# Folding the row maxima of four query tiles at once, one causal mask for both orientations, and smaller tiles for the norm weights, in a hybrid attention block

## The chip, the cores and the metric

The kernel runs on one core of a Trainium2 chip. The time is that of one execution on the device in microseconds; the kernel before was run three times, and the median of the runs counts. One more execution was recorded by the hardware profiler.

## The reference

One layer of a decoder trunk over 2048 tokens of width 1024. A normed input is projected once; its columns feed three attention branches and a gate. The branches' outputs, times the gate, go through one output projection and are added to the input.

```python
h = rms_norm(x, norm_g)
cq, ckv, kr, dq, dk, dv, mq, z = split(h @ w_in)
# A: latent attention, 8 heads, q and k of 64 + 32 (rotary) columns, causal
q = rms_norm(rms_norm(cq, q_norm_g) @ w_uq, qn_g); k = rms_norm(concat(k_nope, kr), kn_g)
a = softmax(where(causal, rope(q) @ rope(k).T / sqrt(96), -1e30)) @ v
# B: differential attention, 4 heads, two maps of 32 columns each, causal
p = softmax(where(causal, q @ k.T / sqrt(32), -1e30))
b = rms_norm((p[0] - lam * p[1]) @ v, subln_g) * (1 - lam_init)
# C: cross-attention to 256 memory tokens, 4 heads
c = softmax(rms_norm(mq, qn_g) @ rms_norm(k_mem, kn_g).T / sqrt(64)) @ v_mem
out = x + (concat(a, b, c) * silu(z)) @ w_out
```

## The kernel before

Everything is computed in tiles of 128 tokens, four of them to a block of 512, four blocks in all. Values that need more precision than 16 bits are kept as a high and a low 16-bit part, so that projections and scores take two or three matmuls each.

The work is cut into **steps**: one per branch, head group and block (`m` for memory, `d` for differential with 2 groups, `a` for latent with 4 groups; 4 blocks each). A step has two parts. Its **preparation** (`prep_m`, `prep_d`, `prep_a`) projects, norms and turns the queries and keys, and ends with an estimate of the row maxima (`est_block`). Its **maps** (class `Map`) then run over key tiles: scores into PSUM on TensorE, exponential on ScalarE (L506), the low part of the probabilities on VectorE (L507), and the product with the values on TensorE (L516, L518, L536).

`est_block` is what the change touches most. For each map of a pair of heads, and for each of four query tiles `t`, it multiplies the queries with the high parts of all keys so far, one block `c` of up to 512 keys at a time (L398). On the diagonal block a second matmul adds the causal mask (L400). From block 1 on (`fold`), ScalarE copies the scores to SBUF in bf16: the first block of keys goes straight to the tile `er` (L404), each later one to a tile `ec` (L407), which VectorE merges into `er` by a maximum (L408). `er` holds two query tiles and has one buffer. After each pair of query tiles VectorE folds the 512 columns to 256, 128 and 64 (L412) and reduces the 64 (L413). When all are there, the maxima are scaled by -1/32 on VectorE (L421) into a spare column of the query tile, which SyncE then turns by a transposing DMA (L484, L900). The scores of the maps read that turned tile, so that the exponential needs no further shift.

```python
                if fold and t % 2:
                    for n in (256, 128, 64):
                        V.tensor_tensor(er[:, :, 0:n], er[:, :, 0:n], er[:, :, n:2 * n], ALU.max)
                    V.reduce_max(mx[:, m, t - 1:t + 1, 0], er[:, :, 0:64], axis=AX.X)
```

Two masks are kept: `mask_t` (keys in rows) is added to the scores of the maps (L575, L921), and `mask_e`, its transpose, to the estimates. Norm weights lie as rows broadcast to all partitions (`gain_row`, L83): `g_mk` and `g_mq` for memory, `g_q` and `g_k` of 96 columns for the latent branch, whose first 64 are only used in a product `g_n`. Small sums and inverse norms (`ss`, and `rstd_of` on GpSimd, L91) have two buffers each; the rotary tables times gain (`rt`) have one.

The order of the instructions on each engine is not that of the program. A loop at the end of the kernel takes the next piece of a preparation, a filling task (gates, latents, output projection) or a map by a table of costs and due times, and gives each a priority. A scheduler with a model of the engines' times then sets the order on each engine, so that an edit in one place can move instructions elsewhere.

## Time and profile before

| | |
|---|---|
| three runs | 1371.38, 1371.22, 1367.65 us; median 1371.22 us |
| profiled execution | 1372.15 us, its span 1370.3 us |
| matmuls on TensorE | busy 94% of the span, weight loads 61% |
| VectorE, ScalarE, GpSimd | busy 82%, 66%, 24% |
| granted TensorE clock | 0.989 of full speed, mean over the span |

The span runs from the first to the last instruction. An engine's share is an average over stages with different limits. The chain of waits follows the work that ended last back to what released it, so its shares say on which engines the end depended; work of an engine that is not on it lay beside other work.

### The profile page before, as it was taken

The numbers are of one execution on the slowest core, as the hardware profiler recorded it, in microseconds if no ns is written. First come the engines' busy times: TensorE is split into PE (matmuls) and PEld (weight loads), VectorE is DVE, ScalarE is ACT, GpSimd is POOL, SyncE is SP. The second block draws the span as 40 slices with busy tenths as digits, with TensorE's granted clock in tenths as the row PEclk, the third lists the DMA queues.
The fourth block names the chain that finished last, engine by engine and source line by source line (L and its number), as shares of the span: only waits on it lengthen the run. The fifth ranks groups of instructions, "written<-read, shape, count | busy, mean of one in ns | idle before, by whom it ended". The sixth has DMA issues, their size and how long they took to land.

```text
span 1370.3 us, 35041 instructions
## 1 busy us (share of the span) xinstructions
PE 1293.0 (94%) x13616; PEld 829.5 (61%) x13616; DVE 1123.1 (82%) x2713; ACT 903.9 (66%) x2163; POOL 333.9 (24%) x477
## 2 busy tenths in 40 slices
PE   5988999999999999999998999999999998999998
PEld 2434556667667767667775656666655665655554
DVE  4657888879889867889899889999998998886745
ACT  6656544677878646786896667677766877665521
POOL 2322232403042133113202143223243323200000
PEclk9999999999999999999999999999999999999999
DMA  7998844223113322447446166347525643275452
GB/s 231 199 208 184 184 111 101 59 60 88 41 25 71 79 34 60 78 110 193 124 98 144 40 167 150 84 107 167 109 71 118 145 99 55 40 155 158 141 184 70
DMA packets 294262, 155.52 MB, mean 113 GB/s; under 512 B 239952, under 2 KB 272848, under 8 KB 294096
## 3 DMA queue, kind: packets, MB, share of 16 engines
q1 hardware_dynamic: 294064, 153.29, 47.7%
q8 instruction: 106, 1.74, 0.5%
q14 instruction: 60, 0.49, 0.1%
q0 software_dynamic: 32, 0.00, 0.0%
HBM read 61.75 MB, written 34.34 MB: 70 GB/s over the span
## 4 chain that ended last, share of the span: by engine, by line
PE 56%; DVE 13%; POOL 9%; ACT 8%; DMA 8%; issue 4%; SPq 1%; ACTq 0%; DVEq 0%; POOLq 0%
PE pp L189 6%; PE pp L187 6%; PE pp L188 6%; PE pe L398 5%; DVE plo L507 4%; PE pv L518 3%; PE pv L516 3%; PE pv L536 3%; PE st L572 3%; PE pp L958 3%; PE pp L959 3%; PE pp L960 3%; PE st L917 3%; PE st L918 2%; PE st L919 2%
## 5 line engine op out<-in xcount | busy, mean ns | idle before, releaser
L506 ACT ACTIVATE p<-st 128x512 f32<-128x512 f32 (+3 forms) x672 | 356.2, 551 | 167.2 <-PE st L919 65.8
L507 DVE TENSOR_TENSOR plo<-p 128x512 f16<-128x512 f32 (+3 forms) x672 | 404.6, 615 | 63.1 <-ACT p L506 59.2
L407 ACT ACTIVATE ec<-pe 128x512 bf16<-128x512 f32 (+3 forms) x384 | 197.2, 536 | 39.2 <-PE pe L400 17.1
L516 PEld LDWEIGHTS <-p 128*128 128x128 bf16 x2304 | 186.0, 99 | 51.5 <-DVE y_a L924 4.7
L518 PEld LDWEIGHTS <-p 128*128 128x128 bf16 x2304 | 173.1, 98 | 39.4 <-issue 4.1
L408 DVE TENSOR_TENSOR er<-er,ec 128x512 bf16<-128x512 bf16 (+3 forms) x384 | 141.5, 378 | 29.9 <-ACT ec L407 15.2
L404 ACT ACTIVATE er<-pe 128x512 bf16<-128x512 f32 x192 | 110.0, 606 | 47.2 <-DVE mx_a L413 18.1
L536 PEld LDWEIGHTS <-plo 128*128 128x128 f16 x2304 | 123.1, 97 | 23.7 <-DVE plo L507 5.8
L917 PE MATMUL st<-qB_a,kT_a 97*128 97x512 f16 (+1 forms) x320 | 112.8, 353 | 13.6 <-ACT p L506 8.7
L516 PE MATMUL pv<-V_d,p 128*128 128x65 f16 x1088 | 116.8, 194 | 3.3 <-DVE y_d L579 2.9
L189 PEld LDWEIGHTS <-ht_x 128*128 128x128 f16 x896 | 87.7, 98 | 52.9 <-ACT ht_x L137 3.9
L188 PEld LDWEIGHTS <-ht_x 128*128 128x128 f16 x896 | 87.8, 98 | 47.8 <-issue 4.0
L518 PE MATMUL pv<-V_d,p 128*128 128x64 f16 x1088 | 116.5, 196 | 0.0
L572 PE MATMUL st<-qB_d,kT_d 97*128 97x512 f16 (+1 forms) x320 | 111.4, 353 | 5.2 <-ACT zc L704 2.1
L187 PEld LDWEIGHTS <-ht_x 128*128 128x128 f16 x896 | 87.7, 98 | 47.1 <-issue 2.8
L516 PE MATMUL pv<-V_a,p 128*128 128x65 f16 x1088 | 112.6, 193 | 2.0 <-DVE y_a L924 1.9
L918 PE MATMUL st<-qB_a,kT_a 96*128 96x512 f16 (+1 forms) x320 | 112.6, 352 | 0.0
L398 PE MATMUL pe<-kT_d,qB_d 96*128 96x512 f16 (+2 forms) x320 | 106.2, 348 | 6.8 <-ACT ec L407 3.6
L518 PE MATMUL pv<-V_a,p 128*128 128x64 f16 x1088 | 112.2, 195 | 0.0
L919 PE MATMUL st<-qB_a,kT_a 96*128 96x512 f16 (+1 forms) x320 | 111.9, 350 | 0.0
L398 PE MATMUL pe<-kT_a,qB_a 96*128 96x512 f16 (+2 forms) x320 | 100.0, 349 | 7.7 <-DMA qB_a<-qs_a 4.6
L189 PE MATMUL pp<-w_d,ht_x 128*128 128x512 f16 x256 | 97.0, 379 | 0.0
(293 smaller groups left out, 3337.7 us busy)
## 6 DMA issues: line engine op xcount, KB each, us to landing
xt_x<-in_x_dram SPq DMA_DIRECT2D x16, 512.0 KB, 4.7
xr<-in_x_dram SPq DMA_DIRECT2D x16, 512.0 KB, 3.6
part<-xr SPq DMA_DIRECT2D x16, 512.0 KB, 2.9
ysc<-yt SPq DMA_DIRECT2D x31, 256.0 KB, 2.3
yl<-ysc SPq DMA_DIRECT2D x15, 512.0 KB, 4.6
zsc<-zc SPq DMA_DIRECT2D x48, 128.0 KB, 2.1
xa<-part SPq DMA_DIRECT2D x12, 512.0 KB, 3.6
out_dram<-xa SPq DMA_DIRECT2D x12, 512.0 KB, 2.9
```

The source lines that it names most:

```text
L187: T.matmul(ps[:, :n], lhsT=ht[:, 0, k], rhs=wt[:, 0, :n], start=(k == 0), stop=False)
L188: T.matmul(ps[:, :n], lhsT=ht[:, 0, k], rhs=wt[:, 1, :n], start=False, stop=False)
L189: T.matmul(ps[:, :n], lhsT=ht[:, 1, k], rhs=wt[:, 0, :n], start=False, stop=(k == NK - 1))
L398: T.matmul(ps[:, 0:n], lhsT=lhs(m, t), rhs=rhs(m, c, n // P), start=True, stop=c < b)
L407: A.activation(ec[:, 0:n], ps[:, 0:n], AF.Copy)
L506: A.activation(p32[:, :n], ps[:, :n], AF.Exp, scale=self.scale)
L507: V.tensor_tensor(plo[:, :n], p32[:, :n], phi[:, :n], ALU.subtract)
L516: T.matmul(pvv[:, t, 0:65], lhsT=phi[:, c], rhs=vt[:, 0:65], start=(j == 0 and t == 0), stop=False, skip_group_check=True)
L518: T.matmul(pvv[:, t, 0:64], lhsT=phi[:, c], rhs=vt[:, 65:129], start=False, stop=False, skip_group_check=True)
L536: last["pv"] = T.matmul(pvv[:, t, 0:65], lhsT=plo[:, c], rhs=vt[:, 0:65], start=False, stop=(j == self.njt - 1), skip_group_check=True)
L572: T.matmul(ps[:, :n], lhsT=st.kTs[j // 4][0:97, h, j % 4, m % 2, :], rhs=st.qB[h][0:97, t0:4, m % 2, :], start=True, stop=not diag)
L917: T.matmul(ps[:, :n], lhsT=kt[0:97, h, j % 4, 0, :], rhs=q[0:97, 0, t0:4, :], start=True, stop=False)
```

## The change

- `er` holds four query tiles instead of two (4 KB a partition instead of 2 KB) and is folded once per map, after its last query tile; the three maxima and the reduction are twice as wide and half as many.
- The scaling of the maxima by -1/32 is done on ScalarE (an activation with a scale) instead of VectorE.
- `mask_e` is gone: on the diagonal block `mask_t` is loaded as weights and the identity is streamed, where the identity was loaded and `mask_e` streamed.
- The memory branch's two gains share one tile, which takes the rotary table's buffer (`rtab`); the latent branch's gains keep only the 32 rotary columns, and the product `g_n` is made from a 64-column row and one in a temporary tile.
- `ss` and the inverse norms of tag `rstd` have one buffer instead of two.

```diff
-    mask_e = cst.tile([P, P], BF16, name="mask_e")
-    make_causal_mask(nc, mask_e, mask_val=NEG)
...
-        r = sm.tile([P, 32 if tag == "rstd" else 8], F32, tag=tag, name=name)
+        r = sm.tile([P, 32 if tag == "rstd" else 8], F32, tag=tag, name=name, bufs=1 if tag == "rstd" else 2)
...
-    g_mk = gain_row(mem_kn_g, 64, "g_mk")
-    g_mq = gain_row(mem_qn_g, 64, "g_mq")
-    V.tensor_tensor(g_mk, g_mk, g_mq, ALU.mult)
+    g_m2 = wk.tile([P, 2, 64], F32, tag="rtab", name="g_m2", bufs=1)
+    SP.dma_start(g_m2[:, 0], mem_kn_g.broadcast_to([P, 64]))
+    SP.dma_start(g_m2[:, 1], mem_qn_g.broadcast_to([P, 64]))
+    g_mk = g_m2[:, 0]
+    V.tensor_tensor(g_mk, g_mk, g_m2[:, 1], ALU.mult)
...
-    g_q = gain_row(mla_qn_g, 96, "g_q")
-    g_k = gain_row(mla_kn_g, 96, "g_k")
-    g_n = cst.tile([P, 64], F32, name="g_n")
-    V.tensor_tensor(g_n, g_q[:, 0:64], g_k[:, 0:64], ALU.mult)
+    g_q = gain_row(mla_qn_g[:, 64:96], 32, "g_q")
+    g_k = gain_row(mla_kn_g[:, 64:96], 32, "g_k")
+    g_n = gain_row(mla_qn_g[:, 0:64], 64, "g_n")
...
+    SP.dma_start(lamw[:, 192:256], mla_kn_g[:, 0:64].broadcast_to([P, 64]))
+    V.tensor_tensor(g_n, g_n, lamw[:, 192:256], ALU.mult)
...
-                if fold and t % 2 == 0:
-                    er = wk.tile([P, 2, 512], BF16, tag="er", name="er", bufs=1)
+                if fold and t == 0:
+                    er = wk.tile([P, 4, 512], BF16, tag="er", name="er", bufs=1)
...
-                        T.matmul(ps[:, t * P:n], lhsT=ident, rhs=mask_e, start=False, stop=True)
+                        T.matmul(ps[:, t * P:n], lhsT=mask_t, rhs=ident, start=False, stop=True)
...
-                        A.activation(er[:, t % 2], ps, AF.Copy)
+                        A.activation(er[:, t], ps, AF.Copy)
...
-                        V.tensor_tensor(er[:, t % 2, 0:n], er[:, t % 2, 0:n], ec[:, 0:n], ALU.max)
+                        V.tensor_tensor(er[:, t, 0:n], er[:, t, 0:n], ec[:, 0:n], ALU.max)
...
-                if fold and t % 2:
-                    for n in (256, 128, 64):
-                        V.tensor_tensor(er[:, :, 0:n], er[:, :, 0:n], er[:, :, n:2 * n], ALU.max)
-                    V.reduce_max(mx[:, m, t - 1:t + 1, 0], er[:, :, 0:64], axis=AX.X)
+            if fold:
+                for n in (256, 128, 64):
+                    V.tensor_tensor(er[:, :, 0:n], er[:, :, 0:n], er[:, :, n:2 * n], ALU.max)
+                V.reduce_max(mx[:, m, :, 0], er[:, :, 0:64], axis=AX.X)
...
-            V.tensor_scalar_mul(mcol(m), mr[:, m, :], -1.0 / MS)
+            A.activation(mcol(m), mr[:, m, :], AF.Copy, scale=-1.0 / MS)
...
-        ss = sm.tile([P, 32], F32, tag="ss", name=f"ss_{nm}")
+        ss = sm.tile([P, 32], F32, tag="ss", name=f"ss_{nm}", bufs=1)
```

The scheduler writes the order anew. Three places follow. The first is VectorE at the end of the first folded estimate of the latent branch (group 0, block 1, first head), `plo` being the low part of the probabilities and `mx` the maxima. Before:

```order
L526 RECIPROCAL rl<-pv 128x4
L412 TENSOR_TENSOR er<-er 128x2x256
L581 TENSOR_SCALAR rl<-rl,neglam 128x4
L412 TENSOR_TENSOR er<-er 128x2x128
L583 SCALAR_TENSOR_TENSOR y_d_11718<-pv,rl,y_d_11718 128x64 x4
L412 TENSOR_TENSOR er<-er 128x2x64
L413 TENSOR_REDUCE mx_a_13330<-er 128x2
L408 TENSOR_TENSOR er<-er,ec 128x384
L408 TENSOR_TENSOR er<-er,ec 128x512
L507 TENSOR_TENSOR plo<-p_12559 128x512
L412 TENSOR_TENSOR er<-er 128x2x256
```

```order
L413 TENSOR_REDUCE mx_a_13330<-er 128x2
L507 TENSOR_TENSOR plo<-p_12696 128x512
L507 TENSOR_TENSOR plo<-p_12720 128x512
L507 TENSOR_TENSOR plo<-p_12738 128x512
L421 TENSOR_SCALAR qs_a_13260<-mx_a_13330 128x4
L507 TENSOR_TENSOR plo<-p_12792 128x512
```

With the change:

```order
L409 TENSOR_TENSOR er<-er,ec 128x512
L584 SCALAR_TENSOR_TENSOR y_d_11594<-pv,rl,y_d_11594 128x64 x4
L508 TENSOR_TENSOR plo<-p_12467 128x512
L413 TENSOR_TENSOR er<-er 128x4x256
L508 TENSOR_TENSOR plo<-p_12482 128x512
L413 TENSOR_TENSOR er<-er 128x4x128
L508 TENSOR_TENSOR plo<-p_12536 128x512
L508 TENSOR_TENSOR plo<-p_12554 128x512
L413 TENSOR_TENSOR er<-er 128x4x64
L508 TENSOR_TENSOR plo<-p_12572 128x512
L508 TENSOR_TENSOR plo<-p_12596 128x512
L414 TENSOR_REDUCE mx_a_13206<-er 128x4
```

The pair's fold before the third query tile is gone and one fold of four tiles stands at the end. The scaling that stood three subtractions behind the last reduction has left this engine.

The second place is ScalarE at the same estimate, from that scaling on, with the change (`p` are the exponentials, `st` the scores, `pe` the estimates):

```order
L507 ACTIVATE p_12596<-st 128x512
L507 ACTIVATE p_12614<-st 128x512
L507 ACTIVATE p_12668<-st 128x512
L507 ACTIVATE p_12689<-st 128x512
L507 ACTIVATE p_12715<-st 128x512
L422 ACTIVATE qs_a_13136<-mx_a_13206 128x4
L405 ACTIVATE er<-pe 128x512 x3
L507 ACTIVATE p_12737<-st 128x512
```

Before, at that place:

```order
L506 ACTIVATE p_12720<-st 128x512
L506 ACTIVATE p_12738<-st 128x512
L506 ACTIVATE p_12792<-st 128x512
L404 ACTIVATE er<-pe 128x512 x2
L506 ACTIVATE p_12813<-st 128x512
```

The scaling now stands in ScalarE's queue between exponentials, and the first copies of the next head's estimate follow it, three at a time instead of two.

The third place is SyncE's queue in the first microseconds, from the second tile of the memory weights `wst_mkv` to the fourth tile of token rows `xt_x`. Before:

```order
L120 DMA wst_mkv_423<-in_w_mem_kv_dram 128x2x512
L314 DMA lamw<-in_diff_lambda_dram 128x128
L78 DMA gq<-in_mla_q_norm_g_dram 128x2x1
L78 DMA gkv<-in_mla_kv_norm_g_dram 128x1
L120 DMA xt_x_239<-in_x_dram 128x1024
```

With the change:

```order
L118 DMA wst_mkv_419<-in_w_mem_kv_dram 128x2x512
L309 DMA g_wo<-in_diff_subln_g_dram 64x1
L312 DMA lamw<-in_mla_kn_g_dram 128x64
L315 DMA lamw<-in_diff_lambda_dram 128x128
L76 DMA gq<-in_mla_q_norm_g_dram 128x2x1
L76 DMA gkv<-in_mla_kv_norm_g_dram 128x1
L118 DMA xt_x_235<-in_x_dram 128x1024
```

Two more issues stand between the weights and the row tile.

## Rows read from the trace of the kernel before

**Rows 1.** The page, busy time and share of the span of each engine.

```profile
PE 1293.0 (94%) x13616; PEld 829.5 (61%) x13616; DVE 1123.1 (82%) x2713; ACT 903.9 (66%) x2163; POOL 333.9 (24%) x477
```

**Rows 2.** Windows: stretch, its length, busy time of PE to POOL, granted clock, DMA.

```profile
0.00:137.00 137.00, 108.80 (x583) 51.59 (x584) 81.97 (x137) 85.65 (x141) 36.44 (x87) 0.98 0.88 205
200.00:600.00 400.00, 391.24 (x4434) 271.56 (x4432) 335.78 (x900) 276.74 (x729) 102.53 (x127) 1.00 0.31 64
600.00:800.00 200.00, 187.04 (x2308) 137.29 (x2306) 178.76 (x442) 150.70 (x380) 47.76 (x65) 0.98 0.49 124
800.00:1000.00 200.00, 197.66 (x2142) 125.81 (x2140) 181.53 (x450) 144.74 (x355) 58.76 (x83) 1.00 0.55 127
1000.00:1200.00 200.00, 182.69 (x2163) 119.53 (x2162) 182.47 (x439) 144.10 (x351) 70.86 (x91) 0.97 0.41 88
200.00:1370.00 1170.00, 1121.25 (x12543) 744.26 (x12540) 986.23 (x2460) 787.04 (x1952) 279.90 (x366) 0.99 0.43 101
```

**Rows 3.** The page, chain of waits that ended last, by engine.

```profile
PE 56%; DVE 13%; POOL 9%; ACT 8%; DMA 8%; issue 4%; SPq 1%; ACTq 0%; DVEq 0%; POOLq 0%
```

**Rows 4.** Waits of PE: us in total, times, longest us.

```profile
PE st L917 <- DMA qB_a<-qs_a: 4.3, 4, 1.5
...
PE pe L398 <- ACT er L404: 3.5, 6, 1.4
```

**Rows 5.** VectorE's groups by form: shapes, count, busy us, mean ns, idle before.

```profile
L412 DVE TENSOR_TENSOR er<-er 128x512 bf16<-128x512 bf16 x96 | 40.5, 422 | 0.8
...
L412 DVE TENSOR_TENSOR er<-er 128x256 bf16<-128x256 bf16 x96 | 28.2, 294 | 0.9
...
L412 DVE TENSOR_TENSOR er<-er 128x128 bf16<-128x128 bf16 x96 | 22.0, 229 | 0.9
...
L413 DVE TENSOR_REDUCE mx_a<-er 128x2 f32<-128x128 bf16 x48 | 13.3, 276 | 0.5
...
L854 DVE TENSOR_REDUCE ss_a<-sqq_a 128x4 f32<-128x256 f32 x16 | 6.5, 406 | 0.1
...
L421 DVE TENSOR_SCALAR qs_a<-mx_a 128x4 f16<-128x4 f32 x32 | 5.7, 184 | 0.2
...
L421 DVE TENSOR_SCALAR s_d<-mx_d 128x4 f16<-128x4 f32 x32 | 5.5, 171 | 0.2
...
L767 DVE TENSOR_TENSOR ql<-ql,rlq 128x1024 f32<-128x1024 f32 x4 | 4.9, 1219 | 1.9 <-POOL rlq L101 1.9
```

**Rows 6.** Line 412: count, ns min/median/max, first and last start.

```profile
L412 DVE TENSOR_TENSOR er<-er x288: 153/283/746, 239.4 to 1285.6; 128x512 bf16<-128x512 bf16 x48, 128x128 bf16<-128x128 bf16 x48, 128x256 bf16<-128x256 bf16 x48
```

**Rows 7.** ScalarE's groups by form.

```profile
L506 ACT ACTIVATE p<-st 128x512 f32<-128x512 f32 x480 | 284.1, 611 | 133.6 <-PE st L919 65.8 <-PE st L572 23.2 <-PE st L921 15.6
...
L596 ACT ACTIVATE ys<-y_d 128x64 f16<-128x64 f32 x64 | 15.8, 263 | 3.6 <-DVE y_d L583 3.5
...
L596 ACT ACTIVATION_READ_ACCUMULATOR ys<-y_d 128x1 f32 x64 | 12.9, 207 | 0.0
```

**Rows 8.** Tile er: who waited for the reductions of line 413 (us, times).

```profile
ACT er L404: 33.2, 31
```

**Rows 9.** The chain of waits, first 60 us: start us, us, what.

```profile
20.21 0.47 SPq L314
...
21.20 0.47 SPq L78
21.70 5.49 DMA xt_x<-in_x_dram
```

**Rows 10.** Lines 101, 242 and 332: count, ns, first and last start.

```profile
L101 POOL TENSOR_TENSOR r_a<-r_a,mhalf x16: 2920/2931/3370, 679.0 to 1180.7; 128x16 f32<-128x16 f32 x16
...
L242 DVE TENSOR_TENSOR mem_kn<-mem_kn,g_mk x1: 684/684/684, 67.6 to 67.6; 128x512 f32<-128x512 f32 x1
...
L332 POOL TENSOR_TENSOR rt_d<-cos_t,g_dk x8: 318/404/4525, 127.0 to 546.6; 128x64 f32<-128x64 f32 x8
```

**Rows 11.** Timeline of GpSimd, first 20 us: the row after its DMA issue.

```profile
6.89 0.23 POOL L97 TENSOR_SCALAR r_x<-ss_x 128x1 f32<-128x1 f32 x1 [3.48 <-ACT xh_x L143]
```

More of the change, by code (lines that the diff above doesn't have):

```diff
@@ L8 @@
 from concourse import mybir
-from concourse.masks import make_causal_mask, make_identity, make_lower_triangular
+from concourse.masks import make_identity, make_lower_triangular
 from concourse._compat import with_exitstack
@@ L623, in prep_m @@
         yield 1.0
-        ss = sm.tile([P, 32], F32, tag="ss", name=f"ss_{nm}")
+        ss = sm.tile([P, 32], F32, tag="ss", name=f"ss_{nm}", bufs=1)
         V.reduce_sum(ss[:, 0:16], sq.rearrange("p t (m d) -> p (t m) d", d=64), axis=AX.X)
@@ L734, in kv_latents @@
             r = rstd_of(ss, [4], f"rlk{b}", "rstd_l")
-            tb = rope_tabs(b, g_k[:, 64:96], f"kr{b}")
+            tb = rope_tabs(b, g_k, f"kr{b}")
             kr = cst.tile([P, 4, 32], F32, name=f"krot{b}")
@@ L825, in prep_a @@
         g, b, nm = st.g, st.b, st.name
-        tb = rope_tabs(b, g_q[:, 64:96], nm)
+        tb = rope_tabs(b, g_q, nm)
         q = new_qkv(f"qkv_{nm}")[:, :, 0:192].rearrange("p t (h d) -> p t h d", d=96)
```

## The prediction

> **What bounds the kernel now.** The first view to read is the page's busy times: TensorE's matmuls are busy for 94% of the span, VectorE for 82%, ScalarE for 66% [rows 1]. One share over the whole span hides that there are stretches, so the windows come next [rows 2]. From 200 to 600 us TensorE is busy 391.2 of 400 us and from 800 to 1000 us 197.7 of 200 us: there it is the bound, and an engine that gets less work gives nothing. From 600 to 800 us it is busy 187.0 us and from 1000 to 1200 us 182.7 us, so it stands still for 13.0 and 17.3 us, 30.3 us together. In these two stretches VectorE is 89% and 91% busy, and the granted clock is 0.98 and 0.97 against 1.00 in the others. A mean of 0.98 means 4% of the time at the lower of the two levels (1.2 GHz instead of 2.4 GHz), so 4 us of work are lost in 200 us; 0.97 loses 6 us; 10 us together, in the stretches where TensorE idled. What the change can win lies there.
>
> The chain of waits says how much of each engine's work sets the end: TensorE 56% of the span, VectorE 13%, ScalarE 8% [rows 3]. VectorE's 13% is 178 us, or 15.9% of its 1123.1 us of work; ScalarE's 8% is 110 us, or 12.1% of its 903.9 us. I use these two as exchange rates: a microsecond of work taken from VectorE is worth 0.159 us of time, one given to ScalarE costs 0.121 us. They are means over the span, and that is the weakest point of the sum. TensorE's own waits behind the touched lines are small: 3.5 us in 6 cases for the first copy of row maxima, 4.3 us in 4 for the transposed queries that follow the maxima [rows 4].
>
> **The fold.** There are 48 folded maps (differential steps 2 groups x 3 blocks x 2 head pairs x 2 maps; latent attention 4 x 3 x 2). Each folded two pairs of query tiles: three maximum operations and one reduction per pair, 422 + 294 + 229 + 276 = 1221 ns, so 2442 ns a map [rows 5]. (The reduction's row is one of two like it, 48 each.) Now each map has one fold of the same elements in half as many instructions. The 512- and 256-element operations are in the rows, 422 and 294 ns; the 1024-element one is not. Between 256 and 512 elements the price rises by 128 ns, so at that slope it costs 422 + 256 = 678 ns. The reduction over 256 elements is next to the 256-element one of the latent preparation, 406 ns [rows 5]. Sum 678 + 422 + 294 + 406 = 1800 ns, 642 ns less per map, 30.8 us in all. From above, the 1024-element operation is bounded by the 1219 ns of a 1024-element f32 multiplication [rows 5]: then 101 ns a map, 4.8 us in all. I take 678, since all three shapes of this very operation lie on nearly one line. Below: if the wider operation cost no more than the 422 ns of its neighbour, 43 us.
>
> **The scaling by -1/32** leaves VectorE: 64 instructions, 5.5 + 5.7 = 11.2 us [rows 5]. VectorE gets 30.8 + 11.2 = 42.0 us less; at 0.159 that is **-6.7 us**. ScalarE gets 64 operations of 4 elements. It has none like it in the trace; the nearest rows are the one-element read of its accumulator, 207 ns, and a 64-element square, 263 ns [rows 7]. I take 207: 13.2 us (upper bound 16.8), at 0.121 **+1.6 us** (+2.0).
>
> **The wait for the tile.** There is one buffer for these maxima, so the first copy of a pair had to wait until the fold of the pair before was read. ScalarE stood idle for that 33.2 us in 31 cases, 1.07 us each [rows 8]. The chances to wait halve, from 96 to 48, but the fold behind them is 0.58 us longer: 15.5 x (1.07 + 0.58) = 25.6 us if each wait lengthens by all of it, 16.6 us if by none. So 8 to 17 us of idle go, at ScalarE's rate 0.9 to 2.0; I take **-1.3 us**. Behind the waiting copy stand exponentials in the same queue, and TensorE waits for those.
>
> **The start.** SyncE's queue gets two DMA issues more. Two gain rows of 96 columns become two of 32, one of 64 for the product and one of 64 in a temporary tile. Where the order on SyncE had three issues between the memory weights and the fourth tile of token rows, it now has five: a load of the subln gain has slid behind those weights, and the temporary one is new. In the chain such an issue is 0.47 us, and the fetch of the row tile, 5.49 us, hangs directly on them [rows 9]. Two more: **+0.9 us**, with 0 as the other end, since TensorE stands still for 28.2 of the first 137 us [rows 2] and later loads may take up the shift.
>
> **Edits at nothing.** The mask product keeps its shape and place; only which operand is loaded as weights is exchanged. The second mask's two operations go from GpSimd, which afterwards waits 3.48 us for ScalarE in any case [rows 11]. The single buffers for sums and inverse norms: GpSimd writes sixteen of the latter between 679.0 and 1180.7 us, one every 33 us [rows 10], and the last reader of one is in the same preparation. The product of memory gains now occupies the rope table's only buffer; it is read at 67.6 us and the first table is written at 127.0 us [rows 10]. If one of these covers went, GpSimd would wait once for one VectorE operation, at most a microsecond or so.
>
> **Clock.** If 7 of TensorE's 48.8 us of idle time after 200 us [rows 2] go, a seventh of the 10 us goes too; I take **-1.0 us**.
>
> Sum: -6.7 + 1.6 - 1.3 + 0.9 - 1.0 = **-6.5 us**. The profiled execution took 1372.15 us, 1370.3 of them span, and lies 0.9 us over the median of 1371.22. From the profiled one the sum gives 1365.7, from the median 1364.7; I say **1365 us**. A measurement of this kernel tells about 0.3%, 4.1 us, from no change: faster is below 1367.1, slower above 1375.3.
>
> **Rival A: full relief.** VectorE itself is the bound in the two loose stretches, and all that it loses there is won. Folds are spread from 239.4 to 1285.6 us [rows 6], so 400 of 1046 us hold 16.1 of the 42.0 us; of the 10 us of clock 16.1/30.3, 5.3 us, return. With the other terms: -16.1 + 1.6 - 1.3 + 0.9 - 5.3 = -20.2 us, 1351 us. For it: 89 and 91% busy. Against it: in the 200 us between, VectorE is as busy (181.5 us) while TensorE hardly idles, so it kept up [rows 2]. The Trainium skill (Perfetto Trace Analysis, Identifying the Most-Contended Engine) says that matmul busy time misleads and that the weight loads' share should be read for TensorE. By that rule VectorE's 82% stands above the weight loads' 61% of the page, and this rival would be the forecast; the stretch from 800 to 1000 us does not agree. I give it 0.12.
>
> **Rival B: hidden anyway.** TensorE's work is unchanged and its order decides. The scheduler has written VectorE's and ScalarE's order anew, and freed slots are filled with work nobody waits for. Only startup and scaling stay, +2.5 us, or the gain is halved, -3: 1368 to 1374 us. For it: 94% busy, and the small waits of rows 4. I give it 0.25.
>
> **Rival C: a later maximum, slower.** The last link before the queries' second transposition gets longer in one place. After the last copy of a map comes a 1.80 us fold instead of a 1.22 us one, and then a scaling in ScalarE's queue, which must wait for VectorE and holds up the exponentials behind it. If it stands behind two exponentials (611 ns each [rows 7]) that it did not stand behind before, each of 64 scalings comes 1.22 + 0.58 = 1.8 us later. At VectorE's rate of 0.159 that is +18.3 us, and with the forecast's other terms +11.8: 1383 us. It decides once ScalarE reaches the scaling before the fold is finished, or once transposed queries arrive after TensorE has run out of older scores. For it: those transposed queries are already waited for. Against it: in the order, before the change the scaling stood behind three VectorE subtractions after the reduction, so it was not prompt either. The Trainium skill (Perfetto Trace Analysis, Optimizing Scalar/DVE Operations) says that where these engines are not saturated but cause bubbles elsewhere, breaking instructions up lets work finish sooner. The change does the reverse, and by that rule this rival would hold from 200 to 600 us, where VectorE is 84% busy; nothing shown yet tells for or against it. I give it 0.18.
>
> **How the numbers follow.** The forecast's own case has 0.45; three quarters of it, all of A and a little of B lie below 1367.1: faster 0.48. Most of B, a quarter of the forecast and the mild form of C lie within: same 0.32. Slower 0.20, from C and from an order that happens to be worse. The range runs from A's 1351 us, which also takes in the fold's cheaper bound, to 1378 us, half way into C. The fold's dear bound (-0.159 x 16.0 = -2.5 instead of -6.7) is 1369 us and lies inside.
>
> **What would show it.** Right: VectorE near 1081 us, ScalarE near 917; ScalarE's idle time before the first copies at 17 to 26 us instead of 33; a 1024-wide fold near 680 ns; TensorE's idle time after 200 us near 42 us and the clock there above 0.97. Wrong: a 1024-wide fold above 900 ns, ScalarE idle before the scalings for more than 20 us, or more waits of TensorE for transposed queries than before. If VectorE's time falls as said and TensorE's idle time does not, B holds.

## The result, and the profile after

The changed kernel takes 1381.91 us (median of five runs, 1376.60 to 1384.57) against 1371.34 us of the kernel before (five runs beside it, 1367.65 to 1373.46). The ratio is 1.0068, with a 95% interval of 1.0040 to 1.0095: **slower**, where 1365 us was forecast. The profiled execution took 1382.26 us.

Two single executions far outside all others, 7252.10 us in the run of the latent gains alone and 2663.93 us in the run of the fold of four in the order of before, are left out of the times below; with them the medians of these two runs would be 1398.43 and 1382.91 us, and later expectations that speak of 1383 us, or of 13.6 us between the two folds, go by the latter.

The page of the kernel after: busy times, and the chain that ended last.

```profile
PE 1297.0 (94%) x13616; PEld 831.1 (60%) x13616; DVE 1095.1 (79%) x2457; ACT 910.9 (66%) x2227; POOL 335.0 (24%) x475
...
PE 58%; DVE 12%; DMA 10%; POOL 8%; ACT 8%; issue 4%; SPq 1%; ACTq 0%; POOLq 0%; DVEq 0%
```

VectorE lost 28.0 us of busy time and ScalarE gained 7.0 [rows 1]. The work moved the way that was forecast, by less than the 42.0 and 13.2 us, yet the span grew by 10.2 us. DMA's share of the chain rose from 8 to 10% [rows 3].

Windows of the kernel after; columns as in [rows 2].

```profile
0.00:137.00 137.00, 106.30 (x546) 49.89 (x547) 78.31 (x130) 83.40 (x136) 33.60 (x83) 0.95 0.86 199
200.00:600.00 400.00, 393.40 (x4458) 271.15 (x4457) 327.15 (x807) 282.26 (x756) 99.11 (x127) 1.00 0.32 65
600.00:800.00 200.00, 187.78 (x2282) 137.32 (x2280) 170.38 (x384) 146.86 (x378) 47.34 (x65) 0.97 0.45 118
800.00:1000.00 200.00, 193.34 (x2058) 122.46 (x2056) 173.29 (x398) 142.69 (x357) 61.92 (x84) 0.98 0.58 130
1000.00:1200.00 200.00, 178.91 (x2097) 118.16 (x2096) 178.29 (x403) 147.19 (x373) 72.46 (x91) 0.97 0.41 91
```

The reader should see that the two loose stretches did not tighten: 187.8 and 178.9 us of TensorE against 187.0 and 182.7 [rows 2]. And a new loose one has appeared from 800 to 1000 us, 193.3 us against 197.7, at a clock of 0.98 instead of 1.00, although VectorE has 8 us less to do there.

VectorE's groups by form, and ScalarE's, of the kernel after (L413 is the old L412, L414 the old L413, L422 the old L421, L405 the old L404).

```profile
L413 DVE TENSOR_TENSOR er<-er 128x1024 bf16<-128x1024 bf16 x48 | 33.0, 688 | 0.4
L413 DVE TENSOR_TENSOR er<-er 128x512 bf16<-128x512 bf16 x48 | 20.5, 428 | 0.3
L413 DVE TENSOR_TENSOR er<-er 128x256 bf16<-128x256 bf16 x48 | 14.3, 298 | 0.3
L414 DVE TENSOR_REDUCE mx_a<-er 128x4 f32<-128x256 bf16 x24 | 9.9, 412 | 0.2
...
L405 ACT ACTIVATE er<-pe 128x512 bf16<-128x512 f32 x192 | 113.7, 612 | 17.7 <-PE pe L399 16.9 <-DVE mx_d L414 0.5
L422 ACT ACTIVATE s_d<-mx_d 128x4 f16<-128x4 f32 x32 | 7.2, 224 | 10.7 <-DVE mx_d L403 6.8 <-DVE mx_d L414 3.9
L422 ACT ACTIVATE qs_a<-mx_a 128x4 f16<-128x4 f32 x32 | 7.1, 223 | 11.2 <-DVE mx_a L414 8.7 <-DVE mx_a L403 2.3
```

Each new operation costs nearly what was forecast: the 1024-wide maximum 688 ns (678 forecast), the reduction 412 (406), the scaling on ScalarE 223 (207). The wait of first copies for the fold went from 33.2 us [rows 8] to 0.5. In its place ScalarE now waits 21.9 us in all before the scalings, 12.6 of them for the fold's reductions (L414) and 9.1 for those of the first block, which is not folded (L403).

The chain of waits of the kernel after, in the start.

```profile
20.89 0.58 SPq L312
...
22.47 0.47 SPq L76
...
22.98 7.44 DMA xt_x<-in_x_dram
```

The row tile is asked for 1.28 us later and takes 7.44 us instead of 5.49 [rows 9]: 3.2 us.

### The profile page after: what moved, and what is told of

Same layout as the page of the kernel before. It is cut to its first block, busy times and chain, and to the rows that moved or that the text cites. A ratio compares the mean times of both kernels' runs of the same rounds, so it can differ in the third digit from the quotient of the medians.

```text
span 1380.5 us, 34936 instructions
## 1 busy us (share of the span) xinstructions
PE 1297.0 (94%) x13616; PEld 831.1 (60%) x13616; DVE 1095.1 (79%) x2457; ACT 910.9 (66%) x2227; POOL 335.0 (24%) x475
## 4 chain that ended last, share of the span: by engine, by line
PE 58%; DVE 12%; DMA 10%; POOL 8%; ACT 8%; issue 4%; SPq 1%; ACTq 0%; POOLq 0%; DVEq 0%
PE pp L187 6%; PE pp L185 6%; PE pp L186 6%; PE pe L399 6%; PE pv L519 4%; PE pv L517 3%; PE pv L537 3%; PE st L573 3%; PE pp L959 3%; DVE plo L508 3%; PE pp L961 3%; PE pp L960 3%; PE st L918 2%; PE st L919 2%; PE st L920 2%
## 5 line engine op out<-in xcount | busy, mean ns | idle before, releaser
L537 PEld LDWEIGHTS <-plo 128*128 128x128 f16 x2304 | 122.1, 98 | 22.1 <-DVE plo L508 8.0
L405 ACT ACTIVATE er<-pe 128x512 bf16<-128x512 f32 x192 | 113.7, 612 | 17.7 <-PE pe L399 16.9
L187 PEld LDWEIGHTS <-ht_x 128*128 128x128 f16 x896 | 87.8, 98 | 55.9 <-issue 5.0
```

The source lines that it names most:

```text
L187: T.matmul(ps[:, :n], lhsT=ht[:, 1, k], rhs=wt[:, 0, :n], start=False, stop=(k == NK - 1))
L537: last["pv"] = T.matmul(pvv[:, t, 0:65], lhsT=plo[:, c], rhs=vt[:, 0:65], start=False, stop=(j == self.njt - 1), skip_group_check=True)
```

## The experiments

Each ratio is to the kernel before on the same chip (its median was 1371.3 to 1373.9 us on the chips used), so two runs are best compared by their ratios. First the edits alone, each in the order that the scheduler then wrote.

**The scaling alone** (the kernel before with this edit):

```diff
-            V.tensor_scalar_mul(mcol(m), mr[:, m, :], -1.0 / MS)
+            A.activation(mcol(m), mr[:, m, :], AF.Copy, scale=-1.0 / MS)
```

> The kernel before with the scaling of the maxima on ScalarE alone. If the later maximum is what costs (theory: the scaling in ScalarE's queue delays the transposed queries, TensorE runs dry and its clock falls), this kernel is 6 to 10 us slower than the one before by itself. If the start (two more DMA issues) or the wide fold is the cause, it stays within 3 us of the kernel before, VectorE about 11 us and ScalarE about 14 us apart from it.

Measured 1382.12 us, ratio 1.0084 (1.0052 to 1.0117): as slow as the whole change, and as the theory of the later maximum had it; the run with the order held, further down, gives another reason.

**The room alone** (one mask, single buffers, the two memory gains in the rope table's tile, latent gains reloaded and trimmed; fold and scaling as before):

> The kernel before with the room-making alone: one mask, shared and trimmed tiles of the norm weights, single buffers; fold and scaling as before. If the start is the cause, TensorE's work runs 3 to 4 us late from 50 us on and the whole is 3 to 5 us slower. If the fold or the scaling is the cause, it is within 2 us of the kernel before.

Measured 1399.20 us, ratio 1.0206 (1.0174 to 1.0237): slower than the whole change, and far above both expectations.

**The change without the scaling** (the diff above, undone in the changed kernel):

> The changed kernel with the scaling put back on VectorE (fold of four tiles and all room-making stay). If the scaling in ScalarE's queue makes it slow, this is about 6 to 10 us faster than the changed kernel, near 1372 to 1375 us. If the start and the fold do, it stays within 3 us of the changed kernel's 1382.

Measured 1395.51 us, ratio 1.0188 (1.0156 to 1.0220): neither expectation.

**The start restored** (the changed kernel; the latent gains come as two full rows, so that SyncE has as many loads ahead of the row tile as before):

```diff
-    g_q = gain_row(mla_qn_g[:, 64:96], 32, "g_q")
-    g_k = gain_row(mla_kn_g[:, 64:96], 32, "g_k")
-    g_n = gain_row(mla_qn_g[:, 0:64], 64, "g_n")
...
+    SP.dma_start(lamw[:, 256:352], mla_qn_g.broadcast_to([P, 96]))
+    SP.dma_start(lamw[:, 384:480], mla_kn_g.broadcast_to([P, 96]))
...
+    G.tensor_copy(g_q, lamw[:, 320:352])
+    G.tensor_copy(g_k, lamw[:, 448:480])
```

> The changed kernel with only its start put right: the latent gains are loaded as two full rows of 96 into the temporary tile and the parts copied out by GpSimd, so that SyncE has as many loads ahead of the fourth row tile as before the change. If the start is the cause, TensorE is 3 to 4 us earlier from 50 us on and the whole is 3 to 5 us faster than the changed kernel, about 1378. If later idle stretches and the clock take it back (each fall of the clock in the trace loses 1.7 us), less of it is seen at the end, and the idle time of TensorE between 750 and 1120 us decides.

Measured 1379.41 us, ratio 1.0051 (1.0029 to 1.0072). The order is nearly that of the changed kernel (47 of 13,616 matmuls stand elsewhere), so the start costs some 2.5 us by the medians. The two intervals overlap (1.0040 to 1.0095 for the changed kernel), but in the profiled executions TensorE is 2.2 us earlier at 140 us and still at the end. It is not the 10.

The parts do not add up: +10 for the scaling and +27 for the room, but +23 for room and fold, and +10 for all three. So the suspicion fell on what every edit changes besides its own work: the order. A comparison of the orders written showed that three of the four room edits move nothing on TensorE and ScalarE, and that the reloading of the latent gains, a few loads at 20 us, moves 6564 matmuls, the first of them the 3367th. The next runs follow from that.

**Room edits that keep the order** (all but the latent gains):

> The kernel before with three of the four room-making edits: one causal mask, the two memory gains in the rope table's tile, single buffers for sums and inverse norms. The four loads of latent gains stay as they were. In the rows that the scheduler wrote, TensorE's and ScalarE's are word for word those of before, VectorE's and SyncE's have 2 moved at the start, GpSimd's lose the second mask. Theory O (the order that the scheduler writes makes the difference, not the edits' own waits): no change, 1368 to 1376 us, ratio 0.997 to 1.003. Theory W (a smaller room makes engines wait for buffers, which was the +27 us of the run with all four edits): at least +10 us, 1382 to 1400 us, with GpSimd or VectorE waiting for a single-buffered sum or inverse norm.

Measured 1371.68 us, ratio 0.9995 (0.9977 to 1.0012). Single buffers, one mask and the shared tile cost nothing that can be measured.

**The latent gains alone**:

> The kernel before with only the latent gains reloaded (two loads of 32 columns, one of 64, one of 64 in a temporary tile); two masks, double buffers and folds as before. Its rows stand in the same order as in the run with all four room-making edits, which took 1399 us; against before, 6564 of TensorE's matmuls stand elsewhere. Theory O (order): it takes what all four took, 1393 to 1402 us. Theory W (waits for buffers): only the later fourth row tile is left, 3 us: 1372 to 1379 us. If it is 1372 to 1379 and the run with three edits is as before too, the edits act only together and both theories fall.

Measured 1397.31 us, ratio 1.0177 (1.0127 to 1.0226): all of the room's cost, within the intervals. VectorE's work is nearly the same as before (1124.6 us busy), and the loss is far from the edit. Windows of this run:

```profile
200.00:600.00 400.00, 391.75 (x4426) 271.31 (x4424) 335.57 (x899) 276.40 (x726) 95.59 (x127) 1.00 0.30 64
600.00:800.00 200.00, 184.37 (x2258) 133.87 (x2256) 172.78 (x420) 144.50 (x360) 52.30 (x63) 0.98 0.47 118
800.00:1000.00 200.00, 189.64 (x2009) 120.96 (x2007) 174.00 (x430) 133.79 (x346) 71.36 (x97) 0.98 0.56 127
1000.00:1200.00 200.00, 180.49 (x2091) 118.71 (x2090) 178.22 (x433) 145.39 (x349) 53.21 (x72) 0.95 0.44 91
```

From 800 to 1000 us TensorE does 189.6 us of work where it did 197.7 [rows 2], with nothing edited there. At equal work of TensorE (columns streamed) this run is 2.3 us behind the kernel before at 545 us, and 25.4 us at 1256.

**The order alone**: no edit but one constant of the planner.

```diff
-    LEAD = 11.0
+    LEAD = 10.5
```

> The kernel before with no edit but one planner constant, the lead by which a step's preparation is due before the step: 10.5 instead of 11.0. Loads, instructions, tiles and buffers are the same; the order is another. Theory O: the time moves by more than this measurement's 0.3%, in either direction, as much as the edits did: between 1360 and 1400 us, more probably slower than before since before's order was the best of the five seen so far. Theory W: order is worth little, 1368 to 1376 us.

> As the run with lead 10.5, with 11.5. Theory O: another time again, between 1360 and 1400 us, and different from the one at 10.5 by more than 4 us if orders scatter. Theory W: 1368 to 1376 us.

Measured 1393.36 us at 10.5, ratio 1.0147 (1.0111 to 1.0183), and 1385.88 us at 11.5, ratio 1.0107 (1.0070 to 1.0144). The order is worth 20 and 13 us here without any change of the work, more than any term of the prediction.

**Works and orders crossed.** To hold the order, edges that fix nothing but the sequence of issue were laid along each engine (`traced` are its instructions as the program names them, `order` a table of places taken from the other kernel):

```python
    for e in ("PE", "DVE", "Activation", "Pool", "SP"):
        mine = [i for i in traced if str(i.engine).split(".")[-1] == e]
        row, order = order[:len(mine)], order[len(mine):]
        for p, q in zip(row, row[1:]):
            tc.add_manual_dep(mine[q], mine[p].name, mybir.DependencyInfo(
                mybir.DependencyClass.NoSync, mybir.DependencyReason.DATA), reason="order")
```

> The changed kernel's work, all of it, in the order of before: edges that only fix the issue order chain each engine's instructions in the sequence that the scheduler wrote for before. TensorE's sequence is that of before; the four-tile fold stands where the second pair's fold stood, the scaling where it stood, but in ScalarE's queue; the four gain loads stand where the old two stood. One thing had to differ for that sequence to be possible: the small tiles of maxima rotate by hand in one tile. Theory O (the new order costs, the edits themselves gain): faster than before, 1360 to 1370 us, which is my sum of -6.5 us with the start's later row tile at +3 instead of +0.9. Rival R (the edits themselves cost: the later maximum, the scaling in ScalarE's queue): 1378 to 1388 us, as the changed kernel.

> The opposite swap: fold in pairs and scaling on VectorE, as before, in the order and the room of the changed kernel (the 4 KB tile, one mask, trimmed gains). TensorE's sequence is that of the changed kernel; the fold of the first pair stands right behind its last maximum. Theory O: slower than the changed kernel by what the edits gain, 1384 to 1394 us. Rival R: back to the time of before, 1368 to 1376 us.

> The kernel before with only the scaling moved to ScalarE, chained in the order of before (in its own order this edit took 1382 us). Theory O: no measurable change, 1368 to 1376 us, since 11 us of VectorE's work goes and 13 us of ScalarE's comes. Rival R: 1380 to 1386 us as in its own order, with TensorE waiting more for transposed queries.

Measured: the changed work in the order of before 1386.22 us, ratio 1.0104 (1.0085 to 1.0123); pairs and scaling on VectorE in the order of the changed kernel 1406.61 us, ratio 1.0256 (1.0233 to 1.0280); the scaling alone in the order of before 1369.41 us, ratio 0.9988 (0.9970 to 1.0006). The third is the cleanest: **the same edit takes 1382 us in its own order and 1369 in the old one**, so all of its cost was the order. The first fell out against theory O: with the order of before the changed work is no faster. The second is above the ranges of both theories. The fold had to be looked at by itself.

**The fold, with order and start held.** Three kernels differ in the fold alone (all have the room, the 4 KB tile, the scaling on ScalarE, the order and the start of before; so that the order was possible, the maxima rotate by hand through one small tile, named `mx_a` for both branches). Pairs in the 4 KB tile:

```diff
-            if fold:
-                for n in (256, 128, 64):
-                    V.tensor_tensor(er[:, :, 0:n], er[:, :, 0:n], er[:, :, n:2 * n], ALU.max)
-                V.reduce_max(mx[:, m, :, 0], er[:, :, 0:64], axis=AX.X)
+                if fold and t % 2:
+                    ep = er[:, t - 1:t + 1]
+                    for n in (256, 128, 64):
+                        V.tensor_tensor(ep[:, :, 0:n], ep[:, :, 0:n], ep[:, :, n:2 * n], ALU.max)
+                    V.reduce_max(mx[:, m, t - 1:t + 1, 0], ep[:, :, 0:64], axis=AX.X)
```

> As the run of the changed kernel's work in the order of before, but with the start of before as well: the latent gains come as two full rows, in the places of the two old loads, and GpSimd copies the parts later. In that earlier run (1386 us) VectorE stood 5.2 us for one of the gain loads at 20 us, and 5 us were lost by 140 us against the scaling-only run. Theory F (the one long fold costs: VectorE's later work, ScalarE's queue behind it and then TensorE wait for it): only the start comes back, 1379 to 1384 us. Theory S (the start and the room were all of it): 1364 to 1373 us.

> The same kernel, order and start, with one thing undone: the maxima of four query tiles still share one 4 KB tile, but are folded two query tiles at a time, each pair where before folded it. Theory F: 1364 to 1373 us, as the scaling-only run in this order (1369 us). Theory S: the same as the run with the fold of four, within 4 us.

> Between the runs with the fold of four (1383 us) and with folds in pairs (1369 us), same order and start: the first maximum, 2x256 elements, is taken per pair where before took it, and only the other two and the reduction are taken for four. By the prices measured, VectorE's work per map is 2 x 424 + 422 + 283 + 411 = 1964 ns against 2449 for pairs and 1806 for four, and what stands after a map's last copy 1540 ns against 1225 and 1806. Theory F (the longer last link of each map costs, in proportion): 54% of the way, 1375 to 1379 us. Rival L (the single 128x1024 instruction of 0.69 us stands in the way of short urgent ones): it is gone, 1366 to 1371 us. Rival B (VectorE's busy time decides): below the pairs' time by a few us, 1362 to 1368 us.

Measured: fold of four 1380.38 us, ratio 1.0070 (1.0045 to 1.0096); pairs 1369.35 us, ratio 0.9966 (0.9948 to 0.9984); first maximum per pair, the rest for four, 1373.74 us, ratio 1.0000 (0.9989 to 1.0010). The fold of four saves VectorE 19.6 us of busy time against pairs, and costs 11.0 us by the medians, 14 by the ratios. Rival B of the last expectation (VectorE's busy time decides) falls. The half way lies a third of the way up by the ratios, below theory F's range and above rival L's: the later end and the long instruction were not separated. The reloaded gains, in the same order, cost up to 5 us: with them the fold of four took 1386.22 us, ratio 1.0104, though these two intervals overlap.

One place shows how a delay reaches TensorE there. The page, the windows and the timelines of GpSimd, VectorE, ScalarE and TensorE with the fold of four (of a timeline: start, duration, instruction, idle before):

```profile
PE 1296.5 (94%) x13616; PEld 830.0 (60%) x13616; DVE 1097.7 (79%) x2457; ACT 909.8 (66%) x2227; POOL 342.5 (25%) x477
```

```profile
274.00:278.00 4.00, 2.13 (x11) 1.03 (x11) 3.69 (x12) 3.79 (x13) 0.31 (x1) 0.60 0.65 40
278.00:282.00 4.00, 4.00 (x18) 1.54 (x17) 0.77 (x3) 0.72 (x2) 0.00 (x0) 0.54 0.49 99
```

```profile
258.07 8.17 POOL L99 TENSOR_TENSOR r_d<-r_d,mhalf 128x32 f32<-128x32 f32 x1
...
266.28 0.80 DVE L468 TENSOR_TENSOR qkv_d<-qkv_d,r_d 128x512 f32<-128x512 f32 x1 [2.49 <-POOL r_d L99]
...
272.33 0.81 DVE L423 TENSOR_TENSOR er<-er 128x1024 bf16<-128x1024 bf16 x1
273.06 0.68 DVE L468 TENSOR_TENSOR qkv_d<-qkv_d,r_d 128x512 f32<-128x512 f32 x1
...
273.77 1.33 ACT L476 ACTIVATE s_d<-qkv_d 128x256 f16<-128x256 f32 x4 [3.70 <-DVE qkv_d L468]
...
275.87 0.59 PE L409 MATMUL pe<-kT_d,qB_d 96*128 96x512 f16 x1 [2.93 <-ACT ec L418]
```

The same views of the same place with pairs; last, TensorE's waits from 268 to 282 us:

```profile
PE 1290.9 (95%) x13616; PEld 828.1 (61%) x13616; DVE 1117.3 (82%) x2649; ACT 910.4 (67%) x2227; POOL 327.2 (24%) x477
```

```profile
274.00:278.00 4.00, 4.00 (x46) 2.66 (x45) 3.08 (x10) 2.69 (x8) 0.00 (x0) 1.00 1.09 123
278.00:282.00 4.00, 4.00 (x43) 2.92 (x40) 3.11 (x10) 3.15 (x8) 0.00 (x0) 1.00 0.00 0
```

```profile
257.67 5.68 POOL L99 TENSOR_TENSOR r_d<-r_d,mhalf 128x32 f32<-128x32 f32 x1
...
263.38 0.80 DVE L469 TENSOR_TENSOR qkv_d<-qkv_d,r_d 128x512 f32<-128x512 f32 x1 [0.88 <-POOL r_d L99]
...
269.42 0.53 DVE L424 TENSOR_TENSOR er<-er 128x512 bf16<-128x512 bf16 x1
269.88 0.68 DVE L469 TENSOR_TENSOR qkv_d<-qkv_d,r_d 128x512 f32<-128x512 f32 x1
...
270.59 1.34 ACT L477 ACTIVATE s_d<-qkv_d 128x256 f16<-128x256 f32 x4 [2.03 <-DVE qkv_d L469]
```

```profile
PE pe L409 <- ACT ec L418: 1.0, 1, 1.0
```

Behind the maximum VectorE has a product that ScalarE waits for (273.06 us); behind ScalarE's four copies stands a copy that empties an estimate's buffer in PSUM; TensorE waits for that buffer. ScalarE waits 3.70 us instead of 2.03, TensorE 2.93 instead of 1.0, and then the granted clock is 0.60 and 0.54 over 8 us (0.54 is nearly all of it at 1.2 GHz instead of 2.4) where it stayed at 1.00. Matched matmul by matmul, TensorE is 1.3 us behind the run with pairs when it comes to this place and 5.6 us behind it, of 19.1 us between these two executions at the end.

But the wide maximum is little of that delay. The product comes 3.18 us later than with pairs, and 2.90 us of it are there before the maximum, at the product of 266.28 against 263.38 us. That one waited for an inverse norm of GpSimd, an instruction that took 8.17 us instead of 5.68. The maximum adds the other 0.3 us (0.73 us from its start to the product's, against 0.46). The long inverse norm is no chance of one execution: the other run with the fold of four in this order has it too (8.18 us), and the five runs in this order without that fold have 5.67 to 5.70 us. Why it is longer there, no run here shows; in the changed kernel's own order it took 5.44 us. Nor is the clock the whole: over the span it was 0.989 with the fold of four and 0.988 with pairs.

**The mirror**: the changed kernel, its order held, with the folds in pairs (and the maxima in the hand-rotated tile).

> The changed kernel with one thing undone: folds of two query tiles in the 4 KB tile, and everything else, the order included, as in the changed kernel (1382 us). The fold of the first pair stands right behind its last maximum, that of the second where the fold of four stood. It is the mirror of the pair of runs in the order of before, where the fold of four took 13.6 us more than folds in pairs. Theory I (the fold of four costs by itself, since each map's maximum ends later): folds in pairs are faster here too, 1366 to 1376 us. Theory M (each order suits the durations that it was written for, and any other folding loses in it): slower than the changed kernel, 1386 to 1406 us, since the order of the run with pairs and scaling on VectorE took 1407 us here. Between 1377 and 1385 us neither holds.

Measured 1398.91 us, ratio 1.0193 (1.0159 to 1.0227). Theory I falls, theory M's range holds. With the scaling on ScalarE throughout:

| | order of before (start restored) | order of the changed kernel |
|---|---|---|
| folds in pairs | 1369.35 us | 1398.91 us |
| fold of four | 1380.38 us | 1381.91 us |

Neither way of folding is the better one. Each of these two orders loses with the pieces that it was not written for, wider and fewer or narrower and more: 11.0 and 17.0 us (14 and 17 by the ratios). Where the other pieces stand in an order had to be chosen by hand, and no other places were tried; and the changed kernel itself was run without edges and hand-rotated tile. That pieces fit their order is a reading of these four times, not shown instruction by instruction.

**Other orders written for the same works.**

> The changed kernel with the planner's lead at 10.5 instead of 11.0: the same work in another order of the scheduler's own. The kernel before took 1393 us at this lead. If the edits gain where the scheduler writes the order for them (my sum, -6.5 us): 1383 to 1390 us or less. If the edits cost 10 us whatever the order: 1399 to 1407 us. If the order is all: anywhere from 1365 to 1400 us, with no fixed distance to before.

> The changed kernel with the planner's lead at 11.5; the kernel before took 1386 us there. If the edits gain: 1376 to 1382 us or less. If they cost 10 us whatever the order: 1392 to 1400 us. If the order is all: anywhere from 1365 to 1400 us, with a distance to before unlike that at 10.5 and 11.0.

> The changed kernel with the start restored, and with folds of two query tiles in the 4 KB tile, in the order that the scheduler writes for it. With the fold of four the same kernel took 1379 us in its own order. If the wide fold costs its 13 us in any order: 1362 to 1370 us. If the scheduler's own order had already absorbed it: 1375 to 1400 us, by the scatter of orders.

Measured: the changed kernel 1403.56 us at 10.5, ratio 1.0229 (1.0192 to 1.0267), and 1383.33 us at 11.5, ratio 1.0087 (1.0056 to 1.0119); folds in pairs with start restored, in their own order, 1396.17 us, ratio 1.0149 (1.0113 to 1.0184), against 1379.41 us of the fold of four. By the ratios, the distance of the changed kernel to the kernel before at the same lead is +11 us at 10.5, +9 at 11.0 and -3 at 11.5. The run at 10.5 alone would fit a cost of 10 us whatever the order; that at 11.5 does not. No cost or gain of the edits stands out of the scatter of the orders, from 1371 to 1404 us. That of the kernel before was the best of those the scheduler wrote.

**A version that beats both**: pairs in the 4 KB tile, scaling on ScalarE, room and start as said, in the order of before. 1369.35 us, 0.34% under the kernel before (0.16 to 0.52%) and 12.6 us under the changed one. The gain is small, and it hangs on a fixed table of places.

## Why the prediction was wrong

**Where the time went.** Each profile's span can be split into TensorE's waits after 200 us (the waits view, all its rows added), the span times what the mean granted clock lacks to 1, and the rest that these two leave.

| run | span | waits | clock | rest |
|---|---|---|---|---|
| before | 1370.3 | 41.7 | 1370.3 x 0.011 = 15.1 | 1313.5 |
| after | 1380.5 | 44.6 | 1380.5 x 0.016 = 22.1 | 1313.8 |
| latent gains alone | 1395.6 | 55.9 | 1395.6 x 0.022 = 30.7 | 1309.0 |
| order of before, fold of four | 1383.4 | 51.0 | 1383.4 x 0.011 = 15.2 | 1317.2 |
| order of before, pairs | 1364.3 | 38.7 | 1364.3 x 0.012 = 16.4 | 1309.2 |
| order of changed, pairs | 1397.9 | 57.4 | 1397.9 x 0.020 = 28.0 | 1312.5 |

The changed kernel's 10.2 us are 2.9 of waits and 7.0 of clock in these two executions. The clock of one kernel varies, 0.982 to 0.993 over the runs of before, and the rest differs by up to 8.2 us between these runs, so the split is rough; over the five runs of the changed kernel the clock was 0.980 to 0.986. At equal work of TensorE (columns streamed) the changed kernel is 4.2 us behind at 200 us, 2.1 at 600, 8.0 at 800, 13.1 at 1100 and 10.3 at 1256. Spread over so many places, no single wait of the changed kernel explains it, and none is named.

**The step that failed** is the exchange rate: "a microsecond of work taken from VectorE is worth 0.159 us of time, one given to ScalarE costs 0.121 us". It takes the order as given. The scheduler wrote another, and the difference between two orders is several times the whole sum. With the order held the rate fails too: the fold of four took 19.6 us from VectorE against pairs, and the kernel became 11.0 us slower by the medians, where the rate has it 3.1 faster.

Point by point:

- **The fold and the scaling, -6.7 us.** The prices of the pieces were right, but 42.0 us of them became 28.0 of busy time. VectorE's durations (count times mean, all groups added) come to 1286.6 us before and 1247.9 after, a difference of 38.7, while its busy time is 163.5 and 152.8 us less than these sums, since an instruction's row overlaps the next by some 60 ns (163.5 us over 2713 instructions). Fewer instructions overlap less. The Trainium skill (Perfetto Trace Analysis, Optimizing Scalar/DVE Operations) says that the write-acknowledgement half of a profiled instruction's latency overlaps with the next instruction; the trace agrees that rows overlap, with these 60 ns.
- **Scaling on ScalarE, +1.6.** For the edit alone, -11.2 x 0.159 + 1.6 = -0.2 us was implied; with the order held it measured 0.9988 (0.9970 to 1.0006), which agrees.
- **The wait for the tile, -1.3.** The wait went further than forecast, to 0.5 us of 33.2, and 21.9 us of new waits before the scalings took its place. What it is worth in time was not measured by itself.
- **The start, +0.9.** It was some 2.5 us by the run with the start restored, and up to 5 us in the order of before. The two issues came as said; that the transfer itself takes 1.95 us longer was left out.
- **Edits at nothing.** Right for the mask, the single buffers and the shared tile (0.9995). Wrong for the reloaded gains, which were counted as two issues and nothing more: 24 us alone. Where the order was held they cost up to 5 us, so most of the 24 is the order.
- **Clock, -1.0.** A seventh of 10 us would have been 1.4. The idle time hardly went (TensorE stands still for 47.8 instead of 48.8 us from 200 to 1370 us, where 42 was forecast), so neither did its clock.
- **The signs named beforehand.** Of the signs of being wrong, ScalarE's 21.9 us before the scalings came; the 1024-wide fold stayed under 900 ns, and TensorE's waits for transposed latent and differential queries fell from 10.3 to 7.8 us. VectorE's time fell and TensorE's idle time did not, which was named as rival B's sign; B's time, 1368 to 1374 us, did not come.
- **Rival C** has the nearest time of all that were priced, 1383 us, but by luck. Its scaling in ScalarE's queue cost nothing with the order held (0.9988). Its longer fold does cost in the order of before, but there the one place followed shows 0.3 us from the fold itself. In the order written for the changed kernel, folds in pairs are slower still. The rule weighed there (the Trainium skill, Perfetto Trace Analysis, Optimizing Scalar/DVE Operations: instructions of engines that are not saturated but cause bubbles may be broken up, so that work completes sooner) agrees with the order of before, 1369 against 1380 us, and not with the order of the changed kernel, 1399 against 1382.
- **Rival A** rested on VectorE as the most contended engine, by the rule of the Trainium skill (Perfetto Trace Analysis, Identifying the Most-Contended Engine). That section names the share of peak FLOPs beside the weight loads, so the prediction used half of its rule. VectorE's busy time fell by 28 us and the span rose; no run here shows that reading to hold.
- **"An order that happens to be worse"** stood in the chance for slower, with no price. It was the main case, and should have had one: the trace of one order can't give it, but an edit after which 8569 of TensorE's 13,616 matmuls stand elsewhere puts every microsecond of the old trace in doubt.

**Still open**: what in an order makes it good. The runs show that orders differ by 20 us on the same work (1373 to 1393 us), and one place of one of them, not a rule for writing a better one. The changed kernel's 10 us lie within that scatter; which waits make them up is not shown. Whether the later end of the fold, its long instruction or the longer inverse norm on GpSimd does the harm in the order of before was not settled either.

## What to carry to other kernels

Where a scheduler writes the order, an edit is two edits: its work, and a new order for all that follows; compare the orders first, and if they differ, measure how far the order alone scatters (one neutral constant changed, 20 and 13 us here) before any gain of a few microseconds is believed. To price the edit itself, hold the order with edges along each engine, in both orders if possible: here the answers had opposite signs. Busy time saved on an engine that is not the bound was worth nothing by itself here; when two runs share an order, match them instruction by instruction and follow a delay back, past the edited line, before it is put down to the edit.

## What was not expected

A few loads of norm weights at 20 us cost 24 us (25.4 between the profiled executions, 23 of them after 545 us), without touching anything there. VectorE's row durations add up to 163.5 us more than its busy time, so that 38.7 us of durations saved were 28.0 us of engine time. With the fold of four in the order of before an instruction of GpSimd takes 2.5 us longer than with pairs, though the two kernels differ in VectorE's work alone. And the same edges that hold an order did not cost anything that could be measured: the scaling-only kernel with them took 0.9988 of the time of before.
